# Two more block pairs through the seven-product scheme, and the last pass ordered by token tile

## The chip, the core and the metric

The kernel runs on one core of a Trainium2 chip. The metric is the time of the whole launch in microseconds of device time; lower is better. TensorE does the matmuls, VectorE and ScalarE empty PSUM and split operands, GpSimd does small side work, and SP issues most DMAs.

## What is computed

One layer of a decoder block on 512 tokens of width 1024, in float32: norm, one input projection, block-sparse attention and a pooling mixer, output projection; then the MLP, whose down projection is what the change touches, and a final norm.

```python
def reference(x, norm_mix, w_in, w_pool, pool_scale, w_out, norm_mlp, w_up, w_down, norm_final):
    ...
        x = x + jnp.concatenate([a, p], axis=-1) @ w_out[l]
        h = rms_norm(x, norm_mlp[l])
        x = x + jnp.square(jax.nn.relu(h @ w_up[l])) @ w_down[l]
    return rms_norm(x, norm_final)
```

The width of the MLP is 4096, which is 32 blocks of 128 features (NF = 32).

## The kernel before

Every float32 matmul is made of three (`mm3`, L204): each operand is split into a high part (ScalarE's cast) and a low part (VectorE's subtraction, `split_into`, L143), and high x high, high x low and low x high are added up in PSUM.

**The up loop** (L782) goes over the 32 feature blocks f. Each step does 24 matmuls (8 chunks of 128 x 3) into one of 8 PSUM banks, ScalarE's relu (L721) and VectorE's product (L727), and splits the weights that are needed four blocks later. The bank is free once relu and product have read it; the 8 banks go round.

**Pairs.** Blocks 2p and 2p + 1 form a pair p. Seen as 2 x 2 blocks (two token halves x two feature blocks, two feature blocks x two column halves), the down projection of a pair is done with seven products instead of eight, after Winograd's form of Strassen's scheme: 7 products x 2 token tiles x 3 = 42 matmuls instead of 48. It needs sums of activations (`a_sums`, `s4`: slots of `a_p[p]`, then split by `a_split`) and sums of weights (`t_load`, `t_sums`, `t_store`): two weight blocks are loaded, four VectorE instructions and one cast of ScalarE make the sums, and two stores of 512 KB put them into DRAM scratch, from where later loads fetch them. In before 14 of the 16 pairs are treated so (PAIRS = 14). The sums of pair p are made at block 2p + 1. The tiles of `t_load` and those of `a_split` share one pair of tags with two buffers each.

**First sweep** (L826): for each pair the products m1, m6, m7 and m4, each over two token tiles, 24 matmuls, in all 8 banks. Behind it m1, m6 and m7 are copied or subtracted into SBUF (y; L842, L846, L856). **Second sweep** (L867): m2, m5 and m3 in the banks of m1, m6 and m7, 18 matmuls for a pair, while VectorE adds y to x.

**Last pass** (L901): the four blocks 28 to 31, kept apart in `late` and `w_last`, are multiplied directly, token tile by token tile, 24 matmuls a tile. The last tile's right half is cut into 320 and 192 columns. After each half come the residual sum (L896), the squares (L212) and the product with the final norm's weights (L914: VectorE, for the last tile GpSimd); then mean (L216), power (L221, GpSimd), scaling and the output DMAs.

Every engine runs its instructions in the order of the program (`in_program_order`, L39, at the end). `advance` (L767) splits the next raw weight tile and issues the load of the one four further on; SP's queue runs in program order too, so a store that waits for its sums holds the loads behind it.

Of the kernel before, what the change touches and what calls it, by code (L numbers as in the profile page):

```python
# [29 lines left out]
LAST = 4  # L30
LAST_AT = (8, 10, 11, 13)
# [4 lines left out]
PAIRS = 14  # L36
# [14 lines left out]
def hybrid_block(  # L51
# [58 lines left out]
    for p in range(PAIRS):  # L110
        steps.append((1, p, 1))
        if p in LAST_AT:
            steps.append((2, LAST_AT.index(p), 0))
# [5 lines left out]
    for sweep, p, k in steps:  # L119
        if sweep == 2:  # L120
            parts = [(slice(None), rows(2 * PAIRS + p))]
        elif sweep == 0:
# [96 lines left out]
    def rsqrt(ms):  # L219
        rstd = small.tile([P, 1], F32, tag="rstd", name="rstd")  # L220
        nc.gpsimd.tensor_tensor(rstd, ms, mhalf, op=ALU.pow)  # L221
        return rstd
# [490 lines left out]
    late = []  # L713

# [3 lines left out]
    def sqrelu(f, acc, ks=(0, 1)):  # L718
        n = len(ks)
        z = ap.tile([P, T], F32, tag="z", name="z")  # L720
        nc.scalar.activation(z[:, :n * HT], acc, AF.Relu)  # L721
        if f < 2 * PAIRS:
            at_slots = slice(3, 5) if f % 2 else slice(0, 3, 2)
            if n == 1:
                at_slot = (3 + ks[0]) if f % 2 else 2 * ks[0]
                at_slots = slice(at_slot, at_slot + 1)
            nc.vector.tensor_mul(a_p[f // 2][:, at_slots, :], halves(acc), halves(z[:, :n * HT]))  # L727
        else:
            nc.vector.tensor_mul(z, acc, z)
            late.append([sp.tile([P, T], F32R, tag=f"r{k}", name=f"r{k}", bufs=LAST) for k in "hl"])  # L730
            if f < NF - 1:
                split_into(*late[-1], z)
        return z
# [11 lines left out]
    def a_split(p, sweep):  # L745

        a = a_p[p]
        n = 4 - sweep
        hi, lo = [sp.tile([P, 4, HT], F32R, tag=f"a{k}", name=f"a{k}", bufs=2) for k in "hl"]
# [15 lines left out]
    w_last = []  # L765

    def advance():  # L767
        sweep, p, k = steps.pop(0)
        raw, shape = raws.pop(0)
        if sweep == 2:  # L770
            hi, lo = [mp.tile([P, D], F32R, tag=f"wl{k}{p}", name=f"wl{k}{p}") for k in "hl"]
            w_last.append((hi, lo))
        else:
            hi = wp.tile([P] + shape, F32R, tag="whi", name="whi")
            lo = wp.tile([P] + shape, F32R, tag="wlo", name="wlo")
            ready.append((hi, lo))
        split_into(hi, lo, raw)
        load()

    t_load(0)  # L780
    a_s = []
    for f in range(NF):  # L782
        p, odd = divmod(f, 2)
        if odd and p + 1 < PAIRS:
            t_load(p + 1)
# [4 lines left out]
        else:  # L790
            acc = bank()
            up(acc, ready.pop(0))
            z = sqrelu(f, acc)
# [32 lines left out]
    for p in range(PAIRS):  # L826
# [22 lines left out]
        product(m4, a, 2, w, LEFT, first, False)  # L849
        advance()  # L850
        if p == 1:
            split_into(*late[-1], z)
        if p % 2 and p < 8:
            t1_load(p - 1)
    for j in range(2):
        nc.vector.tensor_sub(y[4 + j], y[2 + j], m7[j])  # L856

    def add_y():
        for j in range(2):
            yield nc.vector.tensor_add(x_at(0, j, 0), x_at(0, j, 0), y[j])  # L860
            yield nc.vector.tensor_add(x_at(0, j, 1), x_at(0, j, 1), y[2 + j])
            yield nc.vector.tensor_sub(x_at(1, j, 0), x_at(1, j, 0), y[4 + j])
            yield nc.vector.tensor_add(x_at(1, j, 1), x_at(1, j, 1), y[4 + j])

    m2, m5, m3 = m1, m6, m7
    adds = add_y()
    for p in range(PAIRS):  # L867
        a, first, last = a_s.pop(0), p == 0, p == PAIRS - 1
        if p + 2 < PAIRS:
            s4(p + 2)  # L870
# [3 lines left out]
        if not last:  # L874
# [5 lines left out]
        product(m2, a, 2, w, LEFT, first, False)  # L880
        product(m5, a, 1, t1.pop(p), slice(None), first, last)
        product(m3, a, 0, w, RIGHT, first, False)
        while steps and (steps[0][0] == 2 or steps[0][1] <= p + 3):
            advance()
        if p % 2 and p + 7 < PAIRS:
            t1_load(p + 7)
    for i in range(2):
        for j in range(2):
            nc.vector.tensor_sub(x_at(i, j, 1), x_at(i, j, 1), m5[j])
    accs = [[m1[0], m3[0]], [m1[1], m3[1]], [m4[0], m5[0]], [m4[1], None]]  # L890

    def down(acc, r_s, w, t, cols, first, last):
        mm3(acc, (r_s[0][:, tok(t)], r_s[1][:, tok(t)]), (w[0][:, cols], w[1][:, cols]), first, last)
# [4 lines left out]
    ops = list(zip(late, w_last))  # L898


    for t in range(NT):  # L901
        parts = [(cols, accs[t][k], (t, k) == (2, 1)) for k, cols in enumerate(HALF)]
        if t == NT - 1:
            parts[1:] = [(slice(512, 832), bank()[:, :320], True), (slice(832, 1024), bank()[:, :192], True)]
        ss = small.tile([P, 3], F32, tag="ss", name="ss")
        o = mp.tile([P, D], F32, tag="o", name="o", bufs=2)
        for k, (cols, acc, fresh) in enumerate(parts):
            for n, op in enumerate(ops):
                down(acc, *op, t, cols, fresh and n == 0, n == LAST - 1)
            residual(acc, t, cols)  # L910
            sq = mp.tile([P, T], F32, tag="sq", name="sq", bufs=1)
            squares(x_t[t][:, cols], sq[:, :cols.stop - cols.start], ss, k)
            eng = nc.gpsimd if t == NT - 1 and k < 2 else nc.vector
            eng.tensor_tensor(o[:, cols], x_t[t][:, cols], g_fin[:, cols], op=ALU.mult)  # L914
            if k == 1 and len(parts) == 3:
                nc.gpsimd.tensor_tensor(ss[:, 0:1], ss[:, 0:1], ss[:, 1:2], op=ALU.add)
        if len(parts) == 3:
            ms = mean_of(ss[:, 0:3:2])
        else:
            ms = mean_of(ss)  # L920
        rstd = rsqrt(ms)
        nc.scalar.activation(o[:, HALF[0]], o[:, HALF[0]], AF.Copy, scale=rstd)
        nc.vector.tensor_scalar_mul(o[:, HALF[1]], o[:, HALF[1]], rstd)
        for k, q in ((1, nc.sync), (0, nc.scalar)):
            q.dma_start(out[0, tok(t), HALF[k]], o[:, HALF[k]])
# [29 lines left out]
```

## Time and profile before

| | |
|---|---|
| median of 3 runs | 524.51 us (523.6 to 525.73) |
| the profiled execution | 525.57 us, of it a span of 523.7 us |
| granted TensorE clock | 0.998 |
| TensorE matmul, busy share of the span | 98%, 2411 instructions |
| VectorE / ScalarE / GpSimd | 71% / 47% / 7% |
| DMA | 92.47 MB, mean 177 GB/s |

The span is cut into stages as follows: start, input projection and attention until about 160 us, output projection and the norm until about 190, the up loop until 359.7, the first sweep until 435.8, the second until 495.0, the last pass until 517.3, and 6.4 us for the last tile's norm and its output. Matmul records overlap (each is 0.39 us long where one starts every 0.23 us), so the distance from start to start is what a matmul costs.

### The profile page before, as it was taken

Reading aid. Unit: us, or ns where it says so; the run is one execution under the profiler, and the core shown is the slowest. Engines: PE = TensorE matmul, PEld = TensorE weight load, DVE = VectorE, ACT = ScalarE, POOL = GpSimd, SP = SyncE. Lnnn points to the kernel's source line nnn. Section 1 sums busy time; section 2 is a strip of 40 time slices with the busy share of each in tenths; the row PEclk is TensorE's granted clock in tenths of the full one; section 3 lists DMA queues with packets and bytes.
Section 4 is the critical chain, followed back from the end, with each engine's and each line's share of the span. In section 5 each row is a group of like instructions: output and inputs, shape, how many; then the busy total and the mean of one; then the engine's idle time right before and its main releaser. Section 6 shows DMA issues by size and latency. Waiting matters only on the chain.

```text
span 523.7 us, 6713 instructions
## 1 busy us (share of the span) xinstructions
PE 512.3 (98%) x2411; PEld 427.0 (82%) x2411; DVE 374.3 (71%) x622; ACT 248.3 (47%) x415; POOL 36.5 (7%) x48
## 2 busy tenths in 40 slices
PE   7999999999999999999999999999999998999995
PEld 4888888888788899888888888888888886888884
DVE  3764879889978647777567775676877768978263
ACT  4544586869735435233232332345656554465032
POOL 2310322121100000000000000000000000000002
PEclk9999999999999999999999999999999999999999
DMA  7532141212334117887887878774788754783012
GB/s 264 179 101 60 47 122 45 86 41 87 120 122 120 41 29 253 272 306 247 276 280 238 282 258 270 237 282 152 246 290 292 277 194 141 248 281 115 0 63 100
DMA packets 74052, 92.47 MB, mean 177 GB/s; under 512 B 4257, under 2 KB 49825, under 8 KB 74018
## 3 DMA queue, kind: packets, MB, share of 16 engines
q1 hardware_dynamic: 73440, 90.98, 52.5%
q10 hardware_dynamic: 578, 1.05, 0.5%
q8 instruction: 19, 0.31, 0.2%
q14 instruction: 15, 0.12, 0.1%
HBM read 75.24 MB, written 16.78 MB: 176 GB/s over the span
## 4 chain that ended last, share of the span: by engine, by line
PE 95%; DMA 1%; DVE 1%; issue 1%; ACT 0%; POOL 0%; SPq 0%; POOLq 0%
PE bank L206 28%; PE bank L207 28%; PE bank L208 28%; PE bank L306 5%; PE bank L483 2%; PE bank L435 2%; PE bank L465 2%; DMA wvr<-in_w_in_dram 1%; PE bank L228 1%; DVE cl L489 0%; DVE a L846 0%; ACT whi L144 0%; POOL o L914 0%; SPq L178 0%; DVE cl L532 0%
## 5 line engine op out<-in xcount | busy, mean ns | idle before, releaser
L206 PE MATMUL bank<-hh,whi 128*128 128x512 f32 (+1 forms) x376 | 141.9, 377 | 0.0
L208 PE MATMUL bank<-hh,wlo 128*128 128x512 f32 (+1 forms) x376 | 141.2, 376 | 0.0
L207 PE MATMUL bank<-hl,whi 128*128 128x512 f32 (+1 forms) x376 | 141.2, 376 | 0.0
L145 DVE TENSOR_TENSOR wlo<-raw,whi 128x1024 fp32r<-128x1024 f32 x84 | 103.1, 1228 | 28.1 <-ACT whi L144 25.7
L144 ACT CAST whi<-raw 128x1024 fp32r<-128x1024 f32 x84 | 87.9, 1048 | 31.1 <-PE bank L208 24.2
L206 PEld LDWEIGHTS bank<-hh,whi 128*128 128x128 f32 x376 | 70.8, 188 | 13.6 <-DVE cl L489 0.9
L208 PEld LDWEIGHTS bank<-hh,wlo 128*128 128x128 f32 x376 | 70.8, 188 | 13.0
L207 PEld LDWEIGHTS bank<-hl,whi 128*128 128x128 f32 x376 | 70.8, 188 | 12.4
L206 PE MATMUL bank<-whi,ah 128*128 128x512 f32 x168 | 65.5, 390 | 0.7 <-DVE a L856 0.7
L207 PE MATMUL bank<-wlo,ah 128*128 128x512 f32 x168 | 65.4, 389 | 0.0
L208 PE MATMUL bank<-whi,al 128*128 128x512 f32 x168 | 65.4, 389 | 0.0
L727 DVE TENSOR_TENSOR a<-bank,z 128x512 f32<-128x512 f32 (+1 forms) x31 | 19.7, 636 | 37.2 <-ACT z L721 37.2
L721 ACT ACTIVATE z<-bank 128x512 f32<-128x512 f32 (+1 forms) x35 | 19.6, 559 | 51.9 <-PE bank L208 49.6
L144 ACT CAST ah<-a 128x1024 fp32r<-128x1024 f32 (+1 forms) x28 | 26.4, 941 | 28.1 <-issue 17.8
L145 DVE TENSOR_TENSOR al<-a,ah 128x1024 fp32r<-128x1024 f32 (+1 forms) x28 | 30.4, 1087 | 11.1 <-ACT ah L144 11.1
L206 PEld LDWEIGHTS bank<-whi,ah 128*128 128x128 f32 x168 | 31.5, 188 | 7.6 <-DVE a L856 1.1
L208 PEld LDWEIGHTS bank<-whi,al 128*128 128x128 f32 x168 | 31.5, 188 | 6.7
L207 PEld LDWEIGHTS bank<-wlo,ah 128*128 128x128 f32 x168 | 31.5, 188 | 6.5
L144 ACT CAST rl<-rh 128x512 fp32r<-128x512 f32 x14 | 8.7, 622 | 54.5 <-DVE rh L694 54.5
L221 POOL TENSOR_TENSOR rstd<-ms,mhalf 128x1 f32<-128x1 f32 x12 | 6.6, 550 | 391.9 <-DVE ms L216 391.9
L212 ACT ACTIVATE sq<-x 128x512 f32<-128x512 f32 (+2 forms) x17 | 10.3, 605 | 33.3 <-DVE x L896 19.9
L444 ACT ACTIVATE p<-p,mn 128x128 f32<-128x128 f32 (+3 forms) x32 | 18.0, 561 | 10.2 <-DVE rs L422 5.1
(149 smaller groups left out, 754.9 us busy)
## 6 DMA issues: line engine op xcount, KB each, us to landing
raw<-in_w_up_dram SPq DMA_DIRECT2D x32, 512.0 KB, 6.1
raw<-in_w_down_dram SPq DMA_DIRECT2D x18, 512.0 KB, 3.4
rh<-in_w_down_dram SPq DMA_DIRECT2D x14, 512.0 KB, 3.3
ta<-rh SPq DMA_DIRECT2D x14, 512.0 KB, 7.5
tb<-rl SPq DMA_DIRECT2D x14, 512.0 KB, 6.5
raw<-in_w_down_dram SPq DMA_DIRECT2D x28, 256.0 KB, 3.2
raw<-in_w_in_dram SPq DMA_DIRECT2D x12, 512.0 KB, 3.7
raw<-in_w_out_dram SPq DMA_DIRECT2D x8, 512.0 KB, 3.2
```

Source lines behind the costliest of these rows:

```text
L144: nc.scalar.copy(hi, src)
L145: (sub or nc.vector).tensor_sub(lo, src, as32(hi))
L206: nc.tensor.matmul(acc, lhsT=a[0], rhs=b[0], start=first, stop=False)
L207: nc.tensor.matmul(acc, lhsT=a[0], rhs=b[1], start=False, stop=False)
L208: nc.tensor.matmul(acc, lhsT=a[1], rhs=b[0], start=False, stop=last)
L306: nc.tensor.matmul(acc, lhsT=a, rhs=w, start=n == 0 and kd == 0, stop=n == 2 and kd == KD - 1)
L435: nc.tensor.matmul(by_qi[qi], lhsT=qs[:, tok(qi)], rhs=k[:, :w], start=n == 0, stop=n == 1)
L444: nc.scalar.activation(p[:, :w], p[:, :w], AF.Exp, scale=-1.0, bias=mn, accum_out=sm)
L465: nc.tensor.transpose(part[:, tok(kc)], probs[qi][:, tok(kc)], ident)
L483: nc.tensor.matmul(acc[:, kc * P:], lhsT=v, rhs=pt[n][:, bl, :], start=kc == 0 and n == 0, stop=kc == NT - 1 and n == 1)
L721: nc.scalar.activation(z[:, :n * HT], acc, AF.Relu)
L727: nc.vector.tensor_mul(a_p[f // 2][:, at_slots, :], halves(acc), halves(z[:, :n * HT]))
```

## The change

All 16 pairs go through the seven products (PAIRS = 16); `late`, `w_last` and the third kind of step fall away. The sums of weights are spread over the up loop by `sums_at` (blocks 1, 2, 4, 6, ... 14, 15, 17, ... 29). The store of a pair's sums stands at the head of the next block, the load of the next pair's blocks at the head of the block of the sums. The activation splits of pairs 0 and 1 come at the end of block 30 and at the head of block 31. The slot sums of pair 15 come in step 1 of the first sweep.

In the last step of the first sweep the subtraction of m7 (L856 in before) stands ahead of the second `advance`. The banks of m4 are closed there and added to x with the y values.

In the second sweep the last four pairs (ENDING = 4) do m5 alone; their splits get tiles of their own and are made in steps 8 to 11, four pairs ahead. What is left of them, m2 and m3 for token tiles 0 and 1, is the last pass, tile by tile; the right half of tile 1 goes in 320 and 192 columns into m4's banks. Tiles 2 and 3 need only m5, and their final norms, with that of tile 0, are done between the products, by one VectorE instruction a half (`normed3`: x times the power times the weights). Tile 1 ends like the last tile of before.

```diff
-PAIRS = 14
+PAIRS = NF // 2
+
+ENDING = 4
...
+        if sweep and p >= PAIRS - ENDING:
+            hi, lo = [mp.tile([P, 3, HT], F32R, tag=f"e{k}", name=f"e{k}", bufs=ENDING) for k in "hl"]
+        else:
+            hi, lo = [sp.tile([P, 4, HT], F32R, tag=f"a{k}", name=f"a{k}", bufs=2) for k in "hl"]
...
+    sums_at = {1 + p * (NF - 4) // (PAIRS - 1): p for p in range(PAIRS)}
...
-        if odd and p + 1 < PAIRS:
-            t_load(p + 1)
+        if f - 1 in sums_at:
+            t_store(sums_at[f - 1])
+        if f in sums_at and sums_at[f] + 1 < PAIRS:
+            t_load(sums_at[f] + 1)
+        if f == NF - 1:
+            a_s.append(a_split(1, 0))
...
-        if odd and p < PAIRS:
+        if odd and p < PAIRS - 1:
             a_sums(p)
-            t_sums(p)
-        elif not odd and 0 < p <= PAIRS:
-            t_store(p - 1)
-        if f in (NF - 3, NF - 2):
-            a_s.append(a_split(len(a_s), 0))
+        if f in sums_at:
+            t_sums(sums_at[f])
+        if f == NF - 2:
+            a_s.append(a_split(0, 0))
...
-        product(m4, a, 2, w, LEFT, first, False)
+        product(m4, a, 2, w, LEFT, first, last)
+        if last:
+            for j in range(2):
+                nc.vector.tensor_sub(y[4 + j], y[2 + j], m7[j])
         advance()
         if p == 1:
-            split_into(*late[-1], z)
+            a_sums(PAIRS - 1)
...
-    for j in range(2):
-        nc.vector.tensor_sub(y[4 + j], y[2 + j], m7[j])
...
+            yield nc.vector.tensor_add(x_at(1, j, 0), m4[j], x_at(1, j, 0))
...
+        if 2 * ENDING - 1 <= p < PAIRS - ENDING - 1:
+            s4(p + ENDING + 1)
+        if 2 * ENDING <= p < PAIRS - ENDING:
+            ends.append(a_split(p + ENDING, 1))
+        if p == PAIRS - ENDING - 1:
+            a_s += ends
         w = ready.pop(0)
...
+        if p < PAIRS - ENDING:
+            product(m2, a, 2, w, LEFT, first, False)
+            product(m5, a, 1, t1.pop(p), slice(None), first, last)
+            for j in range(2):
+                one(m3[j], a, 0, j, w, RIGHT, first, j == 1 and p == PAIRS - ENDING - 1)
+        else:
+            product(m5, a, 1, t1.pop(p), slice(None), first, last)
+            ending.append((a, w))
...
+    def normed3(t, rstd, k, o):
+        nc.vector.scalar_tensor_tensor(o[:, HALF[k]], x_t[t][:, HALF[k]], rstd, g_fin[:, HALF[k]], op0=ALU.mult,
+                                       op1=ALU.mult)
+        (nc.sync if k else nc.scalar).dma_start(out[0, tok(t), HALF[k]], o[:, HALF[k]])
...
+    def last_products(t, acc, k, cols, fresh):
+        for n, (a, w) in enumerate(ending):
+            one(acc, a, 0 if k else 2, t, w, cols, fresh and n == 0, n == ENDING - 1)
...
+    o0, o = out_of(), out_of()
+    normed3(t0, r0, 0, o0)
+    nc.gpsimd.tensor_tensor(o[:, LEFT], x_t[t1_][:, LEFT], g_fin[:, LEFT], op=ALU.mult)
+    parts = [(slice(512, 832), m4[0][:, :320]), (slice(832, 1024), m4[1][:, :192])]
+    for n, (cols, acc) in enumerate(parts):
+        last_products(t1_, acc, 1, cols, True)
+        residual(acc, t1_, cols)
+        square(t1_, 1 + n, cols)
+        if n == 0:
+            normed3(t0, r0, 1, o0)
+            nc.gpsimd.tensor_tensor(o[:, cols], x_t[t1_][:, cols], g_fin[:, cols], op=ALU.mult)
+            nc.gpsimd.tensor_tensor(ss[t1_][:, 0:1], ss[t1_][:, 0:1], ss[t1_][:, 1:2], op=ALU.add)
         else:
-            ms = mean_of(ss)
+            nc.vector.tensor_tensor(o[:, cols], x_t[t1_][:, cols], g_fin[:, cols], op=ALU.mult)
...
```

## Rows read from the trace of the kernel before

**Rows 1.** The page, part 4: share of the chain that ended last, by engine.

```profile
PE 95%; DMA 1%; DVE 1%; issue 1%; ACT 0%; POOL 0%; SPq 0%; POOLq 0%
```

**Rows 2.** TensorE's waits by releaser, whole span: total us, times, longest us.

```profile
PE bank L206 <- DVE a L846: 0.7, 1, 0.7
PE bank L206 <- DVE a L856: 0.7, 1, 0.7
```

**Rows 3.** Timeline of TensorE, sweeps and last pass: start us, duration us, engine, line.

```profile
359.69 0.39 PE L206 MATMUL bank<-whi,ah 128*128 128x512 f32 x1
...
436.99 0.39 PE L208 MATMUL bank<-whi,al 128*128 128x512 f32 x1
...
494.99 0.39 PE L206 MATMUL bank<-wlh,rh 128*128 128x512 f32 x1
...
514.03 0.30 PE L206 MATMUL bank<-wlh,rh 128*128 128x320 f32 x1
...
515.79 0.25 PE L206 MATMUL bank<-wlh,rh 128*128 128x192 f32 x1
```

**Rows 4.** Timeline of all engines between the two sweeps.

```profile
437.32 1.28 DVE L846 TENSOR_TENSOR a<-bank,a 128x512 f32<-128x512 f32 x2
...
438.06 0.50 PE L206 MATMUL bank<-t,ah 128*128 128x512 f32 x1 [0.69 <-DVE a L846]
...
441.18 0.95 DVE L145 TENSOR_TENSOR al<-a,ah 128x768 fp32r<-128x768 f32 x1
...
442.36 0.40 PE L208 MATMUL bank<-whi,al 128*128 128x512 f32 x1
```

**Rows 5.** Timeline of the up loop, relu and sums of block 25, relu of 29.

```profile
327.25 0.60 ACT L721 ACTIVATE z<-bank 128x512 f32<-128x512 f32 x1 [3.42 <-PE bank L208]
...
333.32 0.69 DVE L145 TENSOR_TENSOR rh<-rh,rl 128x512 fp32r<-128x512 f32 x1
...
349.01 0.60 ACT L721 ACTIVATE z<-bank 128x512 f32<-128x512 f32 x1 [1.91 <-PE bank L208]
```

**Rows 6.** DMA issues: last stores, all, tile ta: count, KB, us to landing.

```profile
ta<-rh SPq DMA_DIRECT2D x1, 512.0 KB, 4.4
tb<-rl SPq DMA_DIRECT2D x1, 512.0 KB, 5.2
...
ta<-rh SPq DMA_DIRECT2D x14, 512.0 KB, 7.5
...
DMA to landing us min/median/max: 3.0/5.2/8.9
```

**Rows 7.** Timeline at the kernel's start: GpSimd and VectorE, inputs in SBUF.

```profile
9.84 1.27 POOL L278 TENSOR_TENSOR wvl<-wvr,wvh 128x512 fp32r<-128x512 f32 x1 [3.71 <-DVE wvh L274]
...
10.33 1.33 DVE L278 TENSOR_TENSOR wvl<-wvr,wvh 128x512 fp32r<-128x512 f32 x1
```

**Rows 8.** Groups by line and form: busy us, mean ns of one, idle before.

```profile
L145 DVE TENSOR_TENSOR wlo<-raw,whi 128x1024 fp32r<-128x1024 f32 x84 | 103.1, 1228 | 28.1 <-ACT whi L144 25.7 <-DMA raw<-ta 0.3
...
L145 DVE TENSOR_TENSOR al<-a,ah 128x1024 fp32r<-128x1024 f32 x14 | 17.1, 1218 | 0.0
L144 ACT CAST ah<-a 128x1024 fp32r<-128x1024 f32 x14 | 14.6, 1046 | 0.0
...
L145 DVE TENSOR_TENSOR al<-a,ah 128x768 fp32r<-128x768 f32 x14 | 13.4, 957 | 11.1 <-ACT ah L144 11.1
...
L145 DVE TENSOR_TENSOR rh<-rh,rl 128x512 fp32r<-128x512 f32 x14 | 9.7, 693 | 0.0
...
L743 DVE TENSOR_TENSOR a<-a 128x256 f32<-128x256 f32 x14 | 5.9, 418 | 0.0
```

**Rows 9.** Timeline of the last tile's norm: GpSimd's products, VectorE's mean.

```profile
515.10 1.29 POOL L914 TENSOR_TENSOR o<-x,grow 128x512 f32<-128x512 f32 x1 [1.25 <-DVE x L896]
...
516.56 0.87 POOL L914 TENSOR_TENSOR o<-x,grow 128x320 f32<-128x320 f32 x1 [0.17 <-DVE x L896]
...
518.60 0.16 DVE L216 SCALAR_TENSOR_TENSOR ms<-ss 128x1 f32<-128x1 f32 x1 [0.54 <-ACT sq L212]
```

More of the change, by code (lines that the diff above doesn't have):

```diff
@@ L109, in hybrid_block @@
     steps = [(0, p, k) for p in range(PAIRS) for k in range(2)]
[L110 to L113, printed above, removed]
+    steps += [(1, p, 1) for p in range(PAIRS)]
     LEFT, RIGHT = HALF
@@ L763, in t4 @@
         nc.vector.tensor_add(r1[:, LEFT], r1[:, LEFT], r0[:, RIGHT])
-    w_last = []
     def advance():
-        sweep, p, k = steps.pop(0)
+        steps.pop(0)
         raw, shape = raws.pop(0)
[L770 to L776, printed above, removed]
+        hi = wp.tile([P] + shape, F32R, tag="whi", name="whi")
+        lo = wp.tile([P] + shape, F32R, tag="wlo", name="wlo")
+        ready.append((hi, lo))
         split_into(hi, lo, raw)
         load()
+    sums_at = {1 + p * (NF - 4) // (PAIRS - 1): p for p in range(PAIRS)}
     t_load(0)
@@ L873, in hybrid_block @@
                 next(adds, None)
-        if not last:
+        if p + 1 < PAIRS - ENDING:
             a_s.append(a_split(p + 1, 1))
@@ L878, in hybrid_block @@
             mp = ctx.enter_context(tc.tile_pool(name="mp", bufs=1, reuse_waits="tile"))
-        w = ready.pop(0)
[L880 to L883, printed above, removed]
+        if 2 * ENDING - 1 <= p < PAIRS - ENDING - 1:
[4 more added lines that the diff above has]
+            a_s += ends
+        w = ready.pop(0)
+        if p < PAIRS - ENDING:
[6 more added lines that the diff above has]
+            ending.append((a, w))
+        while steps and steps[0][1] <= p + 3:
             advance()
@@ L886, in hybrid_block @@
             t1_load(p + 7)
[L887 to L893, printed above, removed]
     def residual(acc, t, cols):
         nc.vector.tensor_add(x_t[t][:, cols], acc, x_t[t][:, cols])
-    ops = list(zip(late, w_last))
@@ L901, in hybrid_block @@
[L901 to L918, printed above, removed]
-        else:
-            ms = mean_of(ss)
[L921 to L925, printed above, removed]
@@ new lines, in out_of @@
+    def out_of():
+        return mp.tile([P, D], F32, tag="o", name="o", bufs=2)
+    def last_products(t, acc, k, cols, fresh):
+        for n, (a, w) in enumerate(ending):
+            one(acc, a, 0 if k else 2, t, w, cols, fresh and n == 0, n == ENDING - 1)
+    t0, t1_, t2, t3 = range(NT)
+    for t in (t2, t3):
+        square(t, 0, LEFT)
+    for j, t in enumerate((t2, t3)):
+        nc.vector.tensor_sub(x_t[t][:, RIGHT], x_t[t][:, RIGHT], m5[j])
+        square(t, 1, RIGHT)
+    for j in range(2):
+        nc.vector.tensor_sub(x_t[j][:, RIGHT], x_t[j][:, RIGHT], m5[j])
@@ new lines, in hybrid_block @@
+    residual(m3[1], t1_, RIGHT)
+    r2, r3 = scale_of(t2), scale_of(t3)
+    last_products(t0, m2[0], 0, LEFT, False)
+    residual(m2[0], t0, LEFT)
+    square(t0, 0, LEFT)
+    o = out_of()
+    for k in range(2):
+        normed3(t2, r2, k, o)
+    last_products(t0, m3[0], 1, RIGHT, False)
+    residual(m3[0], t0, RIGHT)
+    square(t0, 1, RIGHT)
+    o = out_of()
+    for k in range(2):
+        normed3(t3, r3, k, o)
+    r0 = scale_of(t0)
+    last_products(t1_, m2[1], 0, LEFT, False)
+    residual(m2[1], t1_, LEFT)
@@ L926, in hybrid_block @@
+    rstd = rsqrt(mean_of(ss[t1_][:, 0:3:2]))
+    nc.scalar.activation(o[:, LEFT], o[:, LEFT], AF.Copy, scale=rstd)
+    nc.vector.tensor_scalar_mul(o[:, RIGHT], o[:, RIGHT], rstd)
+    for k, q in ((1, nc.sync), (0, nc.scalar)):
+        q.dma_start(out[0, tok(t1_), HALF[k]], o[:, HALF[k]])
     in_program_order(tc)
```

41 lines of the change are left out of this document (19 added, 22 removed).

## The prediction

> **What bounds the kernel now.** I read the page's chain of waits first: 95% of the span is TensorE [rows 1], at a granted clock of 0.998, which is the higher of its two levels, 2.4 GHz. So only two things can shorten it: fewer matmuls, or fewer moments in which TensorE waits. The list of TensorE's waits shows what there is to win. Outside the start and the attention part, two waits of 0.7 us stand there [rows 2], both between the two sweeps of the down projection. The timeline gives the price of one matmul: from the first of the first sweep at 359.69 to the one at 436.99 there are 341 steps (14 pairs x 24, and m2 of the next pair), so 77.30 / 341 = 0.2267 us each. The last pass confirms it (84 full-width matmuls from 494.99 to 514.03). Its last half tile goes in 12 matmuls of 320 columns, 1.76 us, and 12 of 192 [rows 3].
>
> **Matmuls taken away.** A pair costs 7 products x 2 token tiles x 3 = 42 matmuls, and the two feature blocks done directly cost 48. Blocks 28 to 31 become pairs 14 and 15, so 12 full-width matmuls go. The split into 320 and 192 columns stays, now on tile 1. 12 x 0.2267 = **-2.72 us**, all on the path, because TensorE ends last almost everywhere.
>
> **Between the sweeps.** From 436.99 to the matmul at 442.36 there are 15 steps. Without gaps that is 3.40 us and it took 5.37, so the two gaps cost 1.97 [rows 3, 4]. The first is m5's, whose bank is emptied by L846 at 437.32. The change leaves that order, so it stays. The second is m3's, behind L856, which came after the weight split of `advance`. The change puts L856 ahead of that split, so m3 can follow m5 at once. What is late next is the low half of the activations of pair 1: VectorE works without a break from 437.32 until that subtraction, which starts at 441.18 and takes 0.96 [rows 4, 8]. The change only permutes VectorE's work here, so the low half still ends at 442.14. The matmul that needs it is just the one that started at 442.36; without the second gap it would come at about 441.4 and wait. I take **-0.1**, bounded by 0 and by half of the 1.97, if VectorE turned out not to be the limit.
>
> **Two more pairs to prepare.** Each brings slot sums, weight sums (`t_sums`), two stores and reads of the sums. In the first loop `t_sums` comes every other block as before (twice in two blocks running), and the list of waits names no TensorE wait there [rows 2]. A block needs its weights four blocks after their split, so a delay of a few microseconds costs nothing in mid-loop. If that cover were gone, each microsecond beyond it would count fully. In pair 1 of the first sweep the slot sums of pair 15 replace the split of block 31: three subtractions of 0.42 for one of 0.69 on VectorE, +0.57. Its load per pair there is about 0.69 + 1.22 + 2 x 1.23 = 4.4 us of 24 x 0.2267 = 5.4, so this is covered. In steps 8 to 10 of the second sweep VectorE does a split and an `s4` more: 2 x 0.96 + 2 x 0.42 + 1.23 = 4.0 us of 18 x 0.2267 = 4.1. That is tight but enough, as splits run one pair ahead. I put 0 for these, with 0.5 as the upper bound.
>
> **The last store, where a wait is added.** Pair 15's sums come at block 29, and its tiles share two buffers with the activation splits. `a_split(1, 0)` stands ahead of block 31 and must wait until the two stores of pair 15 have landed. Behind it in ScalarE's queue stands the relu of block 31, behind that VectorE's product, and only then is the bank free in which m4's second tile begins: the 22nd matmul of the sweep, 359.69 + 21 x 0.2267 = 364.45. The sums end 6.76 us after the relu of their block starts (327.25 to 333.32 + 0.69), and for block 29 that is 349.01 + 6.76 = 355.8 [rows 5]. SP's queue holds only one raw load between, which is through by then. The first store then lands at 360.2 (4.4 us, the nearest row: the last store of the kernel before, with the same work around it), the second, issued 0.43 later, at 361.4 (5.2) [rows 6]. The cast (1.05) has ended by then; subtraction (1.22) and product (0.69) end at 363.3 [rows 8], with 1.1 us to spare: **0**. At the median of all 14 stores, 7.5 us, with the second store 0.8 later as above, the same sum gives 366.4 and a stall of 2.0; at the 8.9 of the longest transfer of this tensor, 3.4 [rows 6].
>
> **The tail.** After m5 the last 60 matmuls run tile 0, then tile 1; their weights and splits are ready long before, and the subtractions of m5 and the norms of tiles 2 and 3 lie beside them. What changes at the end is that VectorE now does tile 0's norm (`normed3`, twice) beside GpSimd's products for tile 1. The rows at the kernel's start show what that costs: GpSimd's product ran from 9.84 to 11.11, VectorE's, with both inputs in SBUF as well, started at 10.33 and ended at 11.66, 0.55 after the other, where it takes 0.69 alone [rows 7, 8]. I count from the first 320-column matmul (514.03 in before). `normed3` of tile 0's left half holds GpSimd's first product until about +1.65 instead of +1.07; it takes 1.29 and ends at +2.95. The second `normed3` ends 0.55 later at +3.5, GpSimd's 0.87 for 320 columns follow until +4.4, and VectorE's product for the last 192 columns, wanted at +3.9, ends at +4.7. The mean comes after that, at about +4.95; in before it came at 518.60, +4.57 [rows 9]. So **+0.4**, between 0 (no contention) and +1.0 (GpSimd getting its second product in ahead of `normed3`). From the mean to the end nothing changes.
>
> On this the Trainium skill has a rule that speaks against the change (SBUF — State Buffer, "Who interferes with whom"): a VectorE instruction with two SBUF inputs and a GpSimd instruction that reads SBUF exclude each other for the whole instruction. By that rule `normed3`, a form that no row shows beside GpSimd, behaves like the product above, and the tail costs the 0.4. If that form ran free the tail would cost nothing and the time be 521.7. The row at 10.33 agrees with the rule.
>
> **Sum.** -2.72 - 0.1 + 0 + 0 + 0.4 = -2.4 us. Against the profiled execution (525.57, of it a span of 523.7) that gives 523.2. That execution lies 1.06 above the median of the runs, 524.51, so against the median I predict **522.1**, 0.46% faster.
>
> **Rivals.**
> A: the second gap closes in full (-0.98 for -0.1) and the tail adds 0.3. -2.72 - 0.98 + 0.3 = -3.4: 521.1. For it: the gap is real. Against it: VectorE's unbroken work until 442.14.
> B: the last stores take the usual 7.5 us, a stall of 2.0: -0.4, 524.1. For it: the median. Against it: the stores of the same place took 4.4 and 5.2, when the loads had thinned out.
> C, slower than before: the same place, but the stores come late as well as land slowly. Break-even is a stall of 2.4, which is a first store that lands 7.9 us after 355.8; each microsecond more counts in full. With 8.9 and a microsecond of delay in SP's queue: -2.4 + 4.4 = +2.0, 526.5.
> D: the tail is dearer, +1.0, and pair steps 8 to 10 cost 0.3: 523.0.
> That the change doesn't do what it says would show as matmuls that are not saved; the loop bounds give 12 fewer, and I see no room for that.
>
> **How the numbers follow.** Forecast 0.54, alone between 521.4 and 522.9; A 0.17; B 0.12; C 0.06; D 0.11. The range from 520.8 to 524.5 takes in the forecast, A, D and most of B, and leaves out C and the edges, some 0.15. About 0.5% (2.6 us) is what a measurement of this kernel can tell from no change, so the line lies at 521.9, close to the forecast. Faster by more: 0.38 of the forecast's 0.54 and nearly all of A, 0.37. Slower by more, above 527.1: half of C, 0.04. Within 0.5%: 0.59.
>
> **What would show it.** Right: 24 matmuls per pair at 0.2267 from the start of the sweep, none waiting at its 22nd; a first gap between the sweeps as before, m3 right behind m5, and a new wait on the low half in m2 of pair 1; the mean of tile 1 about 5 us after the first 320-column matmul; GpSimd's products behind VectorE's. Wrong: a TensorE wait on a product of block 31 (B, C), no wait in pair 1 of the second sweep (A), or waits in steps 9 to 12 of the second sweep.

## The result, and the profile after

The changed kernel takes 521.49 us (median of 5 runs, 521.04 to 522.43); the kernel before took 525.65 in the 5 runs set against it (523.6 to 525.73). The ratio is 0.9941, interval 0.9928 to 0.9955, so 0.6% faster. In a second comparison the same two kernels took 521.57 and 524.46, a ratio of 0.9945 (0.993 to 0.996). Forecast were 522.1 and a range from 520.8 to 524.5.

The page's head, TensorE and VectorE rows and the chain of waits of the changed kernel:

```profile
span 519.3 us, 6775 instructions
...
PE 509.3 (98%) x2399; PEld 424.2 (82%) x2399; DVE 385.8 (74%) x638; ACT 251.1 (48%) x416; POOL 37.1 (7%) x48
...
PE 93%; DVE 2%; ACT 1%; DMA 1%; POOL 1%; issue 0%; SPq 0%; POOLq 0%; DVEq 0%; ACTq 0%
```

There are 12 matmuls fewer (2411 before), and TensorE is still what ends last. Its waits by releaser (total us, times, longest us), beside [rows 2]:

```profile
PE bank L194 <- POOL ident masks.py:199: 1.4, 1, 1.4
PE bank L201 <- DVE a L834: 0.7, 1, 0.7
PE bank L203 <- DVE al L140: 0.6, 1, 0.6
PE bank L430 <- DVE cl L484: 0.4, 2, 0.2
PE bank L223 <- DVE xn L284: 0.3, 1, 0.3
```

L834 is the wait for m5's bank, which stayed. The wait for m3's bank is gone, and one for the low half of pair 1's activations ("al") stands in its place. No product of the up loop and no later step of the second sweep is in the list.

Now the stages. TensorE's timeline of the changed kernel, first matmul of the first sweep and first one of 320 columns, beside [rows 3]:

```profile
358.06 0.39 PE L201 MATMUL bank<-whi,ah 128*128 128x512 f32 x1
...
509.60 0.30 PE L201 MATMUL bank<-whi,eh 128*128 128x320 f32 x1
```

| stretch, us | before | after | difference |
|---|---|---|---|
| start to the first matmul of the first sweep | 359.69 | 358.06 | -1.63 |
| from there to the first 320-column matmul | 154.34 | 151.54 | -2.80 |
| from there to the end of the span | 9.67 | 9.70 | +0.03 |

The three add up to the difference of the spans, 523.7 to 519.3. The second line is the change's work; the first is a stretch that the change barely touches and is explained below.

### The profile page after: what moved, and what is told of

Read it like the earlier page. It is cut to its first block, busy times and chain, and to the rows that moved or that the text cites. A ratio compares the mean times of both kernels' runs of the same rounds, so it can differ in the third digit from the quotient of the medians.

```text
span 519.3 us, 6775 instructions
## 1 busy us (share of the span) xinstructions
PE 509.3 (98%) x2399; PEld 424.2 (82%) x2399; DVE 385.8 (74%) x638; ACT 251.1 (48%) x416; POOL 37.1 (7%) x48
## 4 chain that ended last, share of the span: by engine, by line
PE 93%; DVE 2%; ACT 1%; DMA 1%; POOL 1%; issue 0%; SPq 0%; POOLq 0%; DVEq 0%; ACTq 0%
PE bank L201 28%; PE bank L203 28%; PE bank L202 28%; PE bank L301 4%; PE bank L478 2%; PE bank L430 2%; PE bank L460 2%; PE bank L223 1%; DMA wvr<-in_w_in_dram 1%; ACT wvh L269 1%; DVE wlo L140 0%; DVE cl L484 0%; POOL o L948 0%; POOL o L956 0%; ACT xn L207 0%
## 5 line engine op out<-in xcount | busy, mean ns | idle before, releaser
L201 PE MATMUL bank<-hh,whi 128*128 128x512 f32 (+1 forms) x376 | 141.9, 377 | 0.0
L140 DVE TENSOR_TENSOR wlo<-raw,whi 128x1024 fp32r<-128x1024 f32 x90 | 110.4, 1228 | 33.4 <-ACT whi L139 31.4
L139 ACT CAST whi<-raw 128x1024 fp32r<-128x1024 f32 x90 | 94.2, 1049 | 40.4 <-PE bank L203 32.0
L201 PEld LDWEIGHTS bank<-hh,whi 128*128 128x128 f32 x376 | 70.8, 188 | 13.3 <-DVE cl L484 0.9
L203 PE MATMUL bank<-whi,al 128*128 128x512 f32 x176 | 68.6, 390 | 0.6 <-DVE al L140 0.6
L201 PE MATMUL bank<-whi,ah 128*128 128x512 f32 x176 | 68.5, 389 | 0.0
L202 PE MATMUL bank<-wlo,ah 128*128 128x512 f32 x176 | 68.5, 389 | 0.0
L719 DVE TENSOR_TENSOR a<-bank,z 128x512 f32<-128x512 f32 (+1 forms) x35 | 22.5, 643 | 36.0 <-ACT z L714 36.0
L203 PEld LDWEIGHTS bank<-whi,al 128*128 128x128 f32 x176 | 33.0, 188 | 7.9 <-DVE al L140 1.1
L202 PEld LDWEIGHTS bank<-wlo,ah 128*128 128x128 f32 x176 | 33.0, 188 | 6.9
L201 PEld LDWEIGHTS bank<-whi,ah 128*128 128x128 f32 x176 | 33.0, 188 | 6.8
L139 ACT CAST rl<-rh 128x512 fp32r<-128x512 f32 x16 | 10.0, 623 | 54.0 <-DVE rh L689 54.0
```

The lines of the kernel that those rows point to most:

```text
L139: nc.scalar.copy(hi, src)
L140: (sub or nc.vector).tensor_sub(lo, src, as32(hi))
L201: nc.tensor.matmul(acc, lhsT=a[0], rhs=b[0], start=first, stop=False)
L202: nc.tensor.matmul(acc, lhsT=a[0], rhs=b[1], start=False, stop=False)
L203: nc.tensor.matmul(acc, lhsT=a[1], rhs=b[0], start=False, stop=last)
```

## Experiments

All ratios are against the kernel before on the same chip. "Stretch" is the second line of the table. Since the start varies by over a microsecond from one execution to the next, verdicts on one or two microseconds go by stretches, not by spans.

**1. Between the sweeps: which wait ends last.** Three kernels change only the order of work around the last step of the first sweep (VectorE's and ScalarE's, and with `advance` the load that it issues).

The first undoes the one move that the diff makes there (the subtraction of m7 goes back behind the second weight split):

```diff
         product(m4, a, 2, w, LEFT, first, last)
+        advance()
         if last:
             for j in range(2):
                 nc.vector.tensor_sub(y[4 + j], y[2 + j], m7[j])
-        advance()
```

> The changed kernel with one part undone: the subtraction of m7 stands behind the second weight split again, as before the change. Measured on TensorE's timeline from the first matmul of the first sweep to the first 320-column matmul, which took 151.54 us in the changed kernel. Theory (VectorE's unbroken work up to the low half of pair 1 is the limit, emptying the bank earlier only moves the wait): 151.6, two gaps again on m5 and m3 and none on the low half, the time within 0.2 us of the changed kernel. Rival (the earlier emptying is worth the gap that it closes): 152.4 to 152.5, 0.9 us slower than the changed kernel.

Measured: 521.69, ratio 0.9954 (0.9939 to 0.997). The stretch is 151.60 (357.63 to 509.23), 0.06 longer than in the changed kernel, and its list of TensorE's waits has the two old ones again and none on the low half:

```profile
PE bank L201 <- DVE a L834: 0.7, 1, 0.7
PE bank L201 <- DVE a L841: 0.7, 1, 0.7
```

So the move ahead of the split is worth less than 0.1 us: it closed one gap and opened another of the same size. Rival A, by which the second gap closes in full, falls.

The second lets the activation split of pair 1 go ahead of that weight split as well:

```diff
             for j in range(2):
                 nc.vector.tensor_sub(y[4 + j], y[2 + j], m7[j])
+            a_s.append(a_split(1, 1))
         advance()
...
-        if p + 1 < PAIRS - ENDING:
+        if 0 < p < PAIRS - ENDING - 1:
             a_s.append(a_split(p + 1, 1))
```

> The changed kernel with the activation split of pair 1 put ahead of the second weight split of the last step of the first sweep. Same stretch, 151.54 us in the changed kernel. Theory: the low half is ready 1.1 us earlier, the wait on it (0.64 us plus the restart) goes and only m5's gap is left, 150.6 to 150.8. Rival (another wait of the same size stands behind it): 151.4 to 151.6.

Measured: 520.42, ratio 0.9924 (0.9908 to 0.9939); stretch 150.62 (357.76 to 508.38), 0.92 shorter. Only m5's wait is left of the two. The third puts both weight splits of that step behind the emptying of m6 and m7 and behind the split of pair 1 (which again leaves the second sweep):

```diff
         if last:
             for j in range(2):
                 nc.scalar.copy(y[j], m1[j])
-        advance()
+        else:
+            advance()
         if last:
...
                 nc.vector.tensor_sub(y[4 + j], y[2 + j], m7[j])
+            a_s.append(a_split(1, 1))
+            advance()
         advance()
```

> The changed kernel with both weight splits of the last step of the first sweep put behind the emptying of m6 and m7 and behind the activation split of pair 1. Nothing is left out. Theory: m5's bank is free 0.6 us before m5 wants it and the low half 1.7 us before it is wanted, both gaps go, 149.6 to 149.8 us for the stretch that took 151.54, and the whole kernel is 1.8 us faster than the changed one, some 519.7 by its median. Rival (the delayed weight splits are late for pair 2 instead): one wait of TensorE on a weight's low half in step 2 of the second sweep, 150.3 or more.

Measured: 519.99, ratio 0.9914 (0.9899 to 0.9929). VectorE's timeline of this kernel, in which what TensorE waits for comes first and the two weight splits (`wlo`) last:

```profile
445.69 1.28 DVE L835 TENSOR_TENSOR a<-bank,a 128x512 f32<-128x512 f32 x2
...
446.89 1.27 DVE L841 TENSOR_TENSOR a<-a,bank 128x512 f32<-128x512 f32 x2
448.08 0.95 DVE L140 TENSOR_TENSOR al<-a,ah 128x768 fp32r<-128x768 f32 x1
448.95 2.35 DVE L140 TENSOR_TENSOR wlo<-raw,whi 128x1024 fp32r<-128x1024 f32 x2
```

Its list of waits has none between the sweeps, and the stretch is 149.60 (359.03 to 508.63): 1.94 less than in the changed kernel, which is the whole 1.97 of the two gaps of before. The weight splits, 2.35 us of work of which the first now starts some 2.5 us later, delay nothing. In a second comparison it took 520.38, ratio 0.9928 (0.9915 to 0.994), with the same stretch of 149.60:

> The kernel of e3 once more, on the same chip as e9: 520.0 on the scale on which the kernel before takes 524.5, a ratio of 0.9914, with the stretch from the first matmul of the first sweep to the first 320-column matmul 149.6. The first matmul of the first sweep may lie anywhere from 357.6 to 359.1, as in the eight profiles of the changed kernel and its variants so far.

**2. The changed kernel once more**, on the chip of experiment 1.

> The changed kernel once more, beside the others on one chip. Theory: the same inner stretch, 151.5 us; against the kernel before 2.8 us by the profile's inner stretches (ratio 0.9947), and what the first comparison showed beyond that (4.2 us between the medians, 4.4 between the spans) is the start: in the two profiles the first matmul of the first sweep came 1.63 us apart, with the same program up to there. Rival (the start is faster for a reason that belongs to the change): that matmul at 358.1 again, and the kernel before at 359.7.

Measured: 521.57, ratio 0.9945; stretch 151.54 again (358.19 to 509.73). The 4.2 us between the medians of the first comparison are thus more than the change is worth; the steady difference is 2.8 to 2.9.

**3. The price of the added wait.** In this kernel the sums of weights of pair 15 come about 5.6 us later:

```diff
-    sums_at = {1 + p * (NF - 4) // (PAIRS - 1): p for p in range(PAIRS)}
+    sums_at = {1 + p * (NF - 4) // (PAIRS - 1): p for p in range(PAIRS - 1)}
+    sums_at[NF - 2] = PAIRS - 1
...
-        if f in sums_at:
-            t_sums(sums_at[f])
         if f == NF - 2:
             a_s.append(a_split(0, 0))
+        if f in sums_at:
+            t_sums(sums_at[f])
```

(What its text on record calls slot sums are the sums of weights, `t_sums`.)

> The changed kernel with the slot sums of pair 15 taken after the split of pair 0's activations at block 30, instead of after the activations of block 29, and their store issued at the head of block 31; nothing else is moved, and all of the computation is done. It measures the price of the wait that the change adds. Theory of the prediction: the split of pair 0's second tile waits for that store, and behind it stand the relu and the product of block 31, for which the 22nd matmul of the first sweep waits. In the changed kernel's clock the sums end near 359.8 instead of 354.1 and the store lands some 2.6 later (its landing in the changed kernel's trace), the cast takes 1.05, the subtraction 1.22, the product 0.69: the bank is free near 365.4 instead of the 362.82 at which it is wanted, so one TensorE wait of about 2.6 us (2 to 5 if the store lands later) appears on the product of block 31, and the stretch from the first matmul of the first sweep to the first 320-column matmul is 153.5 to 156.5 instead of 151.5. Rival: the store is not what anything on the path waits for (the margin is larger than the chain says, or the bank is not the one wanted): no wait there and 151.5.

Measured: 524.77 (one run), and one TensorE wait more: "PE bank L201 <- DVE a L719: 2.7, 1, 2.7". Its timeline shows the chain link by link: sums, first store, cast behind the first store, subtraction behind the second, product of block 31, matmul.

```profile
359.70 0.69 DVE L140 TENSOR_TENSOR rh<-rh,rl 128x512 fp32r<-128x512 f32 x1
360.42 0.32 SPq L695 DMA_DIRECT2D ta<-rh  x1
...
363.12 1.05 ACT L139 CAST ah<-a 128x1024 fp32r<-128x1024 f32 x1 [3.46 <-DMA ta<-rh]
364.43 1.23 DVE L140 TENSOR_TENSOR al<-a,ah 128x1024 fp32r<-128x1024 f32 x1 [4.04 <-DMA tb<-rl]
365.57 0.68 DVE L719 TENSOR_TENSOR a<-bank,z 128x512 f32<-128x512 f32 x1
366.31 0.50 PE L201 MATMUL bank<-whi,ah 128*128 128x512 f32 x1 [2.66 <-DVE a L719]
```

The stretch is 154.53, 2.99 longer, and nearly all of that is this wait: the step to the matmul that waited takes 3.04 and the next one 0.34, where 0.23 is usual, together 2.9. (The 2.66 are idle time, counted from the end of the last record, 0.39 long.) The theory of the prediction holds, with its place (the 22nd matmul), its chain and its price; the rival falls. This delay would have turned the change into no change at all.

**4. The tail.** First what the changed kernel does there, its timeline beside [rows 9]:

```profile
511.37 1.29 POOL L948 TENSOR_TENSOR o<-x,grow 128x512 f32<-128x512 f32 x1 [1.51 <-ACT sq L207]
511.55 0.49 DVE L895 TENSOR_TENSOR x<-bank,x 128x320 f32<-128x320 f32 x1 [0.40 <-PE bank L203]
511.96 1.25 DVE L907 SCALAR_TENSOR_TENSOR o<-x,rstd,grow 128x512 f32<-128x512 f32 x1
...
512.62 1.31 POOL L956 TENSOR_TENSOR o<-x,grow 128x320 f32<-128x320 f32 x1
513.13 0.34 DVE L895 TENSOR_TENSOR x<-bank,x 128x192 f32<-128x192 f32 x1
513.51 0.63 DVE L959 TENSOR_TENSOR o<-x,grow 128x192 f32<-128x192 f32 x1
513.57 0.36 ACT L207 ACTIVATE sq<-x 128x192 f32<-128x192 f32 x1 [0.87 <-DVE x L895]
...
514.22 0.16 DVE L211 SCALAR_TENSOR_TENSOR ms<-ss 128x1 f32<-128x1 f32 x1
```

The exclusion that the prediction counted is there. `normed3` (L907) starts at 511.96 beside GpSimd's product and ends 0.55 after it, at 513.21, in 1.25 us where it takes 0.74 alone; then GpSimd's 320 columns need 1.31 for 0.87, since they are held until `normed3` is through; then VectorE's 192-column product needs 0.63 for 0.36. By this the Trainium skill (SBUF — State Buffer, "Who interferes with whom") holds for `normed3` too, as the prediction took it to: the trace agrees, with 1.25 us beside GpSimd and 0.74 alone. And yet the mean comes at +4.62, counted from the first 320-column matmul, where before it came at +4.57. (That is this profile; the tail varies from one to the next, as the next section says.) Three kernels ask why.

The first moves the norm of tile 0's right half behind the root of tile 1. (Its text on record describes the move wrongly, as one of the left half to the front; the theories' numbers are those meant.)

```diff
         if n == 0:
-            normed3(t0, r0, 1, o0)
             nc.gpsimd.tensor_tensor(o[:, cols], x_t[t1_][:, cols], g_fin[:, cols], op=ALU.mult)
...
     rstd = rsqrt(mean_of(ss[t1_][:, 0:3:2]))
+    normed3(t0, r0, 1, o0)
```

> The changed kernel with the norm of tile 0's left half moved from the parts of tile 1 to right behind its root, so that VectorE has done it before the first GpSimd product of tile 1; the right half stays where it was. It tests the tail's price. Theory 1, from the changed kernel's trace: the exclusion of VectorE and GpSimd costs the tail's end little, because VectorE's product for the last 192 columns comes at most 0.3 later than it could and ScalarE's square runs beside it: the mean of tile 1 comes 4.3 to 4.6 us after the first 320-column matmul (4.62 in the changed kernel), and the time falls by 0 to 0.3. Theory 2, the prediction's term: the exclusion costs the tail 0.4 or more, all of which goes: the mean at +4.2 or earlier, and 0.4 or more off the time. In both GpSimd's first product starts earlier than 1.77 us after the first 320-column matmul and its second, for 320 columns, takes 0.87 again.

Measured: 521.93, ratio 0.9958 (0.9944 to 0.9972), no gain. But the profile shows two effects that cancel:

```profile
512.54 0.86 POOL L955 TENSOR_TENSOR o<-x,grow 128x320 f32<-128x320 f32 x1
512.81 0.36 DVE L895 TENSOR_TENSOR x<-bank,x 128x192 f32<-128x192 f32 x1 [0.83 <-PE bank L203]
513.21 0.41 DVE L958 TENSOR_TENSOR o<-x,grow 128x192 f32<-128x192 f32 x1
...
513.83 0.16 DVE L211 SCALAR_TENSOR_TENSOR ms<-ss 128x1 f32<-128x1 f32 x1 [0.21 <-ACT sq L207]
513.91 0.74 DVE L907 SCALAR_TENSOR_TENSOR o<-x,rstd,grow 128x512 f32<-128x512 f32 x1
514.07 0.99 POOL L216 TENSOR_TENSOR rstd<-ms,mhalf 128x1 f32<-128x1 f32 x1 [0.40 <-DVE ms L211]
```

With its first 320-column matmul at 509.54, the mean comes at +4.29, 0.33 sooner. That is what the exclusion costs there, and not `normed3`'s own work: without it VectorE sits idle for 0.83 ahead of the last residual, more than the 0.74 that it takes alone. It is near the 0.4 of the prediction, and the mean lies between the two theories' ranges (4.3 to 4.6, and 4.2 or earlier). That GpSimd's first product would start earlier did not come (+1.76 for +1.77). Then the moved norm excludes GpSimd's root, which takes 0.99 for 0.55, and the last scalings start at +5.55, 0.11 later than in the changed kernel (+5.44).

The second is the kernel before, with VectorE's last product moved behind the mean, to see where the other 0.3 went: in both profiles of before ScalarE's last square starts 0.38 after the residual has ended, in the changed kernel 0.10.

```diff
-            eng.tensor_tensor(o[:, cols], x_t[t][:, cols], g_fin[:, cols], op=ALU.mult)
+            if k < 2:
+                eng.tensor_tensor(o[:, cols], x_t[t][:, cols], g_fin[:, cols], op=ALU.mult)
...
             ms = mean_of(ss[:, 0:3:2])
+            nc.vector.tensor_tensor(o[:, cols], x_t[t][:, cols], g_fin[:, cols], op=ALU.mult)
```

> The kernel before with one move: VectorE's product of the last 192 columns of tile 3 is issued behind the mean instead of ahead of it; nothing else is moved. In both profiles of the kernel before, ScalarE's square of those columns starts 0.38 after the residual has ended, just when that product ends; in the changed kernel it starts 0.10 after the residual. Theory: in the kernel before the square waited for the product, so the changed kernel's tail gained some 0.28 there, which the prediction did not count, and paid about that much for the exclusion of VectorE and GpSimd, which it did count. Then here the square starts 0.1 after the residual and the mean comes 4.2 to 4.3 us after the first 320-column matmul instead of 4.57. Rival: the square's late start is not the product's doing; the mean stays at 4.5 to 4.6, and the exclusion cost the changed kernel next to nothing.

Measured (523.99, one run):

```profile
515.75 0.36 DVE L896 TENSOR_TENSOR x<-bank,x 128x192 f32<-128x192 f32 x1 [0.83 <-PE bank L208]
...
516.49 0.36 ACT L212 ACTIVATE sq<-x 128x192 f32<-128x192 f32 x1 [0.92 <-DVE x L896]
...
517.05 0.16 DVE L216 SCALAR_TENSOR_TENSOR ms<-ss 128x1 f32<-128x1 f32 x1 [0.94 <-ACT sq L212]
```

The square still starts 0.38 after the residual (516.11 to 516.49), and the mean comes at +4.58. My theory falls: the product does not hold the square. The 0.28 are there in all three profiles of the old tail and in none of the eleven of the new one and its variants, but what causes them is open.

The third has both halves of tile 0's norm ahead of GpSimd's first product:

```diff
     normed3(t0, r0, 0, o0)
+    normed3(t0, r0, 1, o0)
     nc.gpsimd.tensor_tensor(o[:, LEFT], x_t[t1_][:, LEFT], g_fin[:, LEFT], op=ALU.mult)
...
         if n == 0:
-            normed3(t0, r0, 1, o0)
```

> The changed kernel with the norm of tile 0's right half moved up to right behind that of its left half, ahead of GpSimd's first product of tile 1; nothing else is moved. Theory (VectorE and GpSimd exclude each other, so what counts is what the pair has to do between the end of tile 0's root and the mean): the second norm takes 0.74 instead of 1.25, GpSimd's first product ends near +3.1 counted from the first 320-column matmul and its second, 0.87 long, near +4.0, after which GpSimd adds two sums (0.3): VectorE's last product is held for at most 0.4 and the mean comes at +4.3 to +4.45 instead of +4.62; the root takes 0.55 again, and the last two scalings start at +5.1 to +5.3 instead of +5.44. Rival (the order among the two engines does not matter, their sum does): the mean stays at +4.6 and the scalings at +5.4.

Measured: 521.93 (one run). The second norm runs in its 0.74 and the 320 columns in 0.87; the mean comes at +4.47 and the last scalings at +5.30 (510.62 to 515.09 and 515.92), 0.15 and 0.14 sooner. GpSimd's second product ends at +4.18 rather than +4.0, so the mean is 0.02 outside the theory's range, the scalings at its end; the rival (4.6 and 5.4) falls.

**5. Put together.** The order between the sweeps of experiment 1 with the first of the tails:

> The order of e3 (both weight splits of the last step of the first sweep behind the emptying of m6 and m7 and behind the split of pair 1's activations) and the tail of e6 in one kernel. If the two are independent, the gain of e3 over the changed kernel (1.5 us) and that of e6 (0 to 0.3 by theory 1, 0.4 or more by theory 2) add: 519.7 to 520.0 by theory 1 or 519.5 by theory 2, on the scale on which the kernel before takes 524.5. Stretch from the first matmul of the first sweep to the first 320-column matmul: 149.6 as in e3.

Measured: 520.42, ratio 0.9921 (0.9907 to 0.9935), stretch 149.60: the tail of this kernel brings nothing, as in experiment 4 (the mean comes at +4.52 in its profile, where GpSimd's first product starts at +2.12 and not at +1.76). With the last of the tails:

> The order between the sweeps of e3 and the tail of e8 in one kernel. Stretch from the first matmul of the first sweep to the first 320-column matmul 149.6 as in e3, and behind it the tail of e8: 0.15 to 0.3 less than e3 if the theory of e8 holds, the same as e3 if its rival does. On the scale on which the kernel before takes 524.5: 519.7 to 520.0.

Measured: 519.45, ratio 0.9911 (0.9898 to 0.9925), stretch 149.60 (359.15 to 508.75), last scalings at +5.31. It is the best kernel of the study, 0.9% faster than before. Against the third kernel of experiment 1 on the same chip it is 0.9 us ahead in the medians; the profiles explain 0.14 of that, and the rest is within what these runs scatter.

**6. The start.** The first profiles differ by 1.63 us ahead of the first sweep. Is that the change?

> The kernel before once more, for the part ahead of the first sweep, which the change leaves alone up to block 27. Theory: where the first matmul of the first sweep lies (359.69 in the first profile of the kernel before, 357.6 to 359.0 in those of the changed kernel and its variants) varies from execution to execution by over a microsecond, and the 1.6 us of difference between the first two profiles are nothing of the change: here it may lie anywhere from 357.5 to 360. Rival: the change moves it by those 1.6 us, and it lies at 359.3 or later again. In both the stretch from there to the first 320-column matmul is 154.3 as in the first profile.

Measured: 525.46, its first matmul at 359.62 and a stretch of 154.31. That alone would speak for the rival, but the kernel with the moved product in experiment 4 has the program of before up to its last microseconds, and its first matmul lies at 358.16. In the eleven profiles of the changed kernel and its variants it lies between 357.63 and 359.32. What moves it, as far as the timelines show, is the landing of an early weight load (`wvr`), for which VectorE's first cast waits. Kernel before again, moved product, and changed kernel:

```profile
8.77 0.76 DVE L274 CAST wvh<-wvr 128x512 fp32r<-128x512 f32 x2 [1.93 <-DMA wvr<-in_w_in_dram]
```
```profile
7.42 0.76 DVE L274 CAST wvh<-wvr 128x512 fp32r<-128x512 f32 x2 [0.59 <-DMA wvr<-in_w_in_dram]
```
```profile
7.53 0.76 DVE L269 CAST wvh<-wvr 128x512 fp32r<-128x512 f32 x2 [0.66 <-DMA wvr<-in_w_in_dram]
```

The cast starts 1.35 apart in the first two, whose programs are the same up to the tail, and their sweeps 1.46 apart. (It isn't this cast alone: in the last kernel of experiment 5 it starts at 7.61, while ScalarE's cast of another part of `wvr` starts at 9.57, 0.74 later than in the changed kernel, and the sweep at 359.15.) So the start varies from execution to execution, and the 1.63 are no part of the change's worth.

## Why the prediction was right, and which step was off

**Matmuls taken away: right.** -2.72 of the -2.80 in the stretch.

**Between the sweeps: right, in mechanism and in size.** The timeline of the changed kernel, beside [rows 4]:

```profile
446.24 0.39 PE L203 MATMUL bank<-whi,al 128*128 128x512 f32 x1
...
446.57 1.28 DVE L834 TENSOR_TENSOR a<-bank,a 128x512 f32<-128x512 f32 x2
...
447.31 0.50 PE L201 MATMUL bank<-t,ah 128*128 128x512 f32 x1 [0.68 <-DVE a L834]
...
450.43 0.95 DVE L140 TENSOR_TENSOR al<-a,ah 128x768 fp32r<-128x768 f32 x1
...
451.44 0.50 PE L203 MATMUL bank<-whi,al 128*128 128x512 f32 x1 [0.64 <-DVE al L140]
```

From the emptying of m6 to the end of the low half VectorE takes 4.81 us (446.57 to 451.38); the prediction had 4.82. The 15 steps take 5.20 instead of 5.37, and the next one 0.33 instead of 0.23, together -0.07 for the forecast -0.1. Experiment 1 shows the same from the other side: 0.06 for undoing the move, 0.92 and 1.94 once VectorE's queue is ordered by who is waited for.

**Two more pairs to prepare: right at 0.** No wait of the up loop or of steps 8 to 12 of the second sweep is in the list.

**The last store: right at 0, with the margin too small.** The sums end at 354.13, which is the forecast 355.8 less the 1.63 by which this execution runs ahead. The landing was mis-sized. DMA issues around 354 in the changed kernel, then the cast and the product behind it:

```profile
ta<-rh SPq DMA_DIRECT2D x1, 512.0 KB, 2.6
```
```profile
356.87 1.05 ACT L139 CAST ah<-a 128x1024 fp32r<-128x1024 f32 x1 [1.07 <-DMA ta<-rh]
...
359.37 0.68 DVE L719 TENSOR_TENSOR a<-bank,z 128x512 f32<-128x512 f32 x1
```

It took 2.6, not 4.4 [rows 6]; the product ends at 360.05, and the bank is wanted at 358.06 + 4.76 = 362.82. So 2.8 us were to spare, not 1.1, and experiment 3 agrees: 5.6 us of delay less 2.8 is the stall that was measured. Rivals B and C rested on the 7.5 and 8.9 of the other stores. Those rows did not bear on the changed kernel: in before SP issues most of these stores straight behind two weight loads, and nine of the 14 are held up for 1.6 to 3.0 us in the issue itself, while the change puts the store at the head of a block. Issues on SP's queue (the second figure is how long the issue took), before and after:

```profile
271.43 2.74 SPq L700 DMA_DIRECT2D ta<-rh  x1
```
```profile
271.31 0.33 SPq L695 DMA_DIRECT2D ta<-rh  x1
```

The 16 first stores (`ta`) of the changed kernel have a median of 2.7, the second ones (`tb`) 4.2; in before it was 7.5 and 6.5. Inside the changed kernel the landing goes with the distance to the last load on SP's queue: the four first stores issued less than 1.5 us behind one took 5.96 to 6.52, the ten issued 2.7 us or more behind it 2.62 to 3.83. That the order of issue is the cause is read from the queues; no run tested it alone.

**The tail: the step that was off.** Forecast +0.4; in the first profile +0.05 at the mean and +0.03 at the end. The exclusion was right: it is there, instruction by instruction, and experiment 4 gives it 0.33 at the mean. The chain that the prediction added up, beside what it measured:

| counted from the first 320-column matmul | forecast | measured |
|---|---|---|
| GpSimd's first product starts | +1.65 | +1.77 |
| second `normed3` ends | +3.5 | +3.61 |
| GpSimd's 320 columns end | +4.4 | +4.33 |
| VectorE's last product ends | +4.7 | +4.54 |
| mean starts | +4.95 | +4.62 |

Down to GpSimd's 320 columns the times agree within 0.12. Too dear were the last two links, 0.3 and 0.25 in the forecast and 0.21 and 0.08 on the chip. Seen against before, the 0.33 of the exclusion stand against the 0.28 by which the last square of before started late: +0.05.

The first link has another reason than the one given, and with it the term is no fixed number. GpSimd's first product writes into the one of the two buffers `o` that tile 3's norm has filled, so it must wait until that output is stored. The store of the right half is issued 0.48 ahead of the first 320-column matmul; by the semaphore events of the traces it lands between +1.55 and +1.97, and in all eleven profiles of the changed kernel and its variants GpSimd's product starts 0.21 behind that. (The timeline names ScalarE's square instead. That is done at +1.72 in each of them, so it could hold the product only in the profiles at the low end.) Before, tile 3 took the buffer of tile 1, stored long ago, and the product started at +1.07. Seven of the eleven have the changed kernel's tail (both profiles of it, the three kernels of experiment 1 with the repeat of the third, and experiment 3). In them the mean comes 2.84 to 2.86 behind the start of that product, so it moves with the store: +4.62 to +5.02, median +4.69. The latest is the first kernel of experiment 1, whose first 320-column matmul lies at 509.23:

```profile
511.41 1.28 POOL L948 TENSOR_TENSOR o<-x,grow 128x512 f32<-128x512 f32 x1 [1.93 <-ACT sq L207]
...
514.25 0.16 DVE L211 SCALAR_TENSOR_TENSOR ms<-ss 128x1 f32<-128x1 f32 x1
```

So the tail costs between +0.05 and +0.45 at the mean, with a median of +0.12, and the first profile shows the low end. That the forecast's 0.4 lies inside this is luck: the wait that spreads it was not in the sum. No run gave `o` a third buffer, so what the wait costs in all is open. Rival D, a tail dearer by 1.0, falls; what its steps 8 to 10 would have cost is 0.

Sum, by the first profile: -2.72 - 0.08 + 0.03 = -2.77, which from the median of 524.51 gives 521.7 (521.8 with the median end of the seven tails, +0.10). The forecast's -2.4 differs by the tail alone; the other 0.2 to the measured 521.49 is scatter. It is also by the tail's 0.4 that the forecast fell on the near side of its line of 0.5%, where the result lies just beyond it: the likelier of the two cases named was not the one that came.

## What to carry to other kernels

Emptying one bank ahead of a split gives nothing while the engine that empties it works without a break: add up its work from the first thing that is waited for to the last, and if that sum stays, the gap only changes its name. Order such a queue by who is waited for, and let what has slack (here 2.35 us of weight splits) go last; that was worth 1.94 us, and the move alone 0.06. Where a step's end is compared with that of before, take the old chain apart too: slack in the old one is a term of the sum, like a cost of the new one. And where a change brings two users of a buffer closer together, put the landing of the first one's store into the sum, and read more than one profile: here it spread a term of 0.05 to 0.45.

## What the runs showed of the hardware

- `normed3` (scalar x tensor x tensor, both tensors in SBUF) and a GpSimd instruction keep each other waiting to the end, in both directions and down to one column: 1.25 us for 0.74 on VectorE (1.64 where GpSimd's product had started later), 1.31 for 0.87 on GpSimd, and 0.99 for 0.55 for GpSimd's power of 128 x 1 behind a `normed3`.
- A 512 KB store (`ta`) landed in 2.62 to 3.83 us where SP's last load was issued 2.7 us or more before it, and in 5.96 to 6.52 where it was less than 1.5, in one kernel. In before the median was 7.5, with up to 3.0 of it in the issue on SP's queue.
- A wait of TensorE costs more than its idle time: each of the two gaps of before cost 0.98 us (1.97 for both) for 0.67 to 0.69 of idle time, since the idle time is counted from the end of a record of 0.39 us where a step is 0.23, and the step after the wait takes 0.34.
- A GpSimd product into a buffer whose contents are being stored starts 0.21 us behind the landing of that store (256 KB, 2.03 to 2.45 us after its issue), in eleven profiles of eleven.
- Two programs that are the same up to the tail have their first sweep start at 358.16 and 359.62, by the landing of one early load. Comparing two profiles by their spans would have credited the change with 4.4 us where 2.8 are its own.
